# One of four heavy experts made light, with a new order of expert steps, the final norm ahead of the leftovers, and down-projections by column halves

## The chip, the cores and the metric

The kernel runs on one core of a Trainium2 chip. The metric is the device time of one execution in microseconds, the median of several runs. One more execution was taken with the hardware profiler; its trace gives the durations of single instructions, and its own time stands beside the runs below.

## The reference

Four residual blocks of a network on 256 tokens of width 1024 (float32): retention and a gated feed-forward layer, dilated attention and a second one, a mixed convolution and neighbourhood-attention layer with a third one, and a Fourier layer followed by a mixture of eight experts. A final norm ends it. The part that matters most here is the mixture:

```
logits = h @ w_router + b_router
top_val, top_idx = lax.top_k(logits, 2)            # 2 of 8 experts for each token
gate = softmax(top_val) at top_idx, 0 elsewhere
out = sum over e of gate[..., e] * ((silu(h @ w1[e]) * (h @ w3[e])) @ w2[e])
# w1[e], w3[e]: 1024 x 3584, w2[e]: 3584 x 1024
...
return x * rsqrt(mean(x * x) + 1e-6) * final_g     # after the residual
```

The weights of all eight experts, 352 MB, are read whichever tokens are routed to them.

## The kernel before

**Stages.** `core` runs the layers one after the other with `Net`'s helpers. Tokens are two blocks of 128 rows. Products that must be exact are made of three: a weight or activation is split into a high and a low part in a rounded format (`load` splits weights: ScalarE copies the high part, line 119, VectorE subtracts for the low part, line 120), and high x high, low x high and high x low are summed in PSUM. Every weight is loaded by `load` (line 110) on SyncE's DMA queue, in program order, into a ring of slots; a load waits until the slot's last reader is done.

**`down`** multiplies a hidden activation by the second matrix of a layer: two row blocks by two column halves, four PSUM tiles. The last `TB` = 5 blocks of 128 hidden columns are held back until the last weight is there, and then done row block by row block, with both column halves in turn for each weight. Seven layers' ends use it; four go on to a layer norm (`post_norm`), three to a gated residual with the statistics of the next norm (`gated_residual`).

**The experts.** After routing, tokens are gathered per expert by products with a selection matrix, and results are scattered back the same way. An expert has `FE` = 3584 hidden columns, cut into 7 steps of 512. A step is one `first` (products with w1 and w3, 2 MB each, in "wide" slots: `rawx` twice and `rawy` twice) and, one step later, one `back` (the product with w2, two loads of 1 MB, slots `raw` three times and `x` once). There are two kinds of step:

- *heavy*: a tile of 128 tokens; weights split in two; 48 products in `first` (line 1079), 24 in `back` (line 1119). Splits go into five buffers `w`.
- *light*: a tile of 64 tokens; weights unsplit, TensorE reads the loaded slots in float32: 32 products (line 1067) and 16 (line 1107).

`order_experts` ranks the experts by their number of tokens; expert 0 is always rank 0, since its weights must be asked for before the ranks are known. Ranks below `NH` = 4 are heavy, the others light. SyncE reads the ranks' expert numbers into registers (line 1255) and uses them for the addresses of all later loads. `plan` is the order of the 56 steps: the first two of expert 0, then light and heavy in turn, and light steps at the end. `rank` is called while step 1 is written.

A step with `u == 0` is a change of expert: the tokens of the next expert are gathered in `prepare`, and those of the expert before are scattered in `scatter`. If an expert has more tokens than its tile holds, the leftovers run after the plan: all eight experts again, behind one branch (`s.tc.If`, line 1380) that reads a count in each engine. The final norm and the stores come behind it.

Of the kernel before, what the change touches and what calls it, by code (L numbers as in the profile page):

```python
# [18 lines left out]
F32 = mybir.dt.float32  # L19
F32R = mybir.dt.float32r  # L20
I32 = mybir.dt.int32
AF = mybir.ActivationFunctionType
ALU = mybir.AluOpType
AX = mybir.AxisListType
PSUM = bass.MemoryType.PSUM
DRAM = bass.MemoryType.DRAM

D = 1024
T = 256
FF = 2816  # L30
NE = 8
NH = 4
FE = 3584
ALPHA = 4 ** 0.25
BIG = 1e30
TB = 5
# [16 lines left out]
class Net:  # L53
# [24 lines left out]
    def banks(s, mm, tp, aux):  # L78

        s.psx.close()  # L80
        s.ps, s.psn = s.pool("psum%d" % mm, 1, s.psx, space=PSUM), (mm, tp, aux)

    def mm_tile(s, shape, name="mm"):
        return s.ps.tile(shape, F32, name=name, tag="mm", bufs=s.psn[0])
# [95 lines left out]
    def down(s, x, name, base, nf):  # L180

        hh, hl = x
        po = [[s.mm_tile([128, 512]) for _ in range(2)] for _ in range(2)]
        w = []
        for f in range(nf):
            if f % 2 == 0:
                w += s.load(s.unit_r(name, base + f // 2))
            if f < nf - TB or f == nf - 1:  # L190
                fs = range(nf - TB, nf) if f == nf - 1 else [f]
                for t in range(2):
                    for g in fs:
                        wh, wl = w[g]
                        for i, (a, b) in enumerate(((hh, wh), (hl, wh), (hh, wl))):
                            for c in range(2):
                                s.nc.tensor.matmul(out=po[t][c], lhsT=a[:, g, t * 128:t * 128 + 128],
                                                   rhs=b[:, 0, c * 512:c * 512 + 512],
                                                   start=(g == 0 and i == 0), stop=(g == nf - 1 and i == 2))
        return po  # L200
# [814 lines left out]
    def experts(s, pc, m, plan, ss, rank=None):  # L1015
# [7 lines left out]
        nc = s.nc  # L1023
# [137 lines left out]
        for n, (r, light, _, u) in enumerate(plan):  # L1161
            P, x, po = ready[r]
            g = first(r, light, u, x)
            pms = next(g)
            hid = turn(last[1], last[3]) if last else None
            if pms is None:
                pms = next(g)
            if n == 1 and rank:
                rank()
                if order[True]:  # L1170
                    late = True
            if late is not None and order[late]:
                prepare(*order[late].pop(0))
            late = None
            if u == 6 and order[light]:
                if n + 1 < len(plan) and plan[n + 1][1] == light:
                    prepare(*order[light].pop(0))
                else:
                    late = light
            if last:  # L1180
                s.second(back, spread, scatter, last, hid, None)
            if u == 0:
                po.extend(s.mm_tile([128, 512]) for _ in range(1 if light else 2))
            rows = 64 if light else 128
            sg = s.np.tile([128, 512], F32, name="tm")
            nc.scalar.activation(out=sg[0:rows], in_=pms[0], func=AF.Silu)
            nc.vector.tensor_tensor(out=sg[0:rows], in0=sg[0:rows], in1=pms[1], op=ALU.mult)
            last = r, light, u, sg, po, P
# [34 lines left out]
    def order_experts(s, q, m, posm, gate, iota, tri8):  # L1223


        nc = s.nc
# [35 lines left out]
                nc.vector.tensor_copy(out[:, t, 1:NE], r[:, 1:NE])  # L1262
        cr = q.tile([128, NE], F32, name="cr")
        by_rank(cr, cn)
        nc.vector.tensor_scalar(out=cr[:, NH:NE], in0=cr[:, NH:NE], scalar1=64.0, scalar2=None, op0=ALU.add)
        cf = q.tile([128, 1], F32, name="cf")
        nc.vector.tensor_reduce(out=cf, in_=cr, axis=AX.X, op=ALU.max)
        nc.vector.tensor_copy(m.cnt, cf)
# [1 line left out]
    def moe(s, x):  # L1270
# [5 lines left out]
        with ExitStack() as ctx:  # L1276
# [15 lines left out]
            with ExitStack() as c2:  # L1292
# [63 lines left out]
                m.posm = pk.tile([128, 2, NE], F32, name="posr")  # L1356
                m.gate = pk.tile([128, 2, NE], F32, name="gater")
                m.cnt = pk.tile([128, 1], I32, name="cnt")
                m.idt = pk.tile([128, NE], I32, name="ids")
                m.counts = pk.tile([128, NE], F32, name="cn")  # L1360
                m.ids = [0]
# [5 lines left out]
            heavy = [(r, False, 0, u) for r in range(NH) for u in range(7)]  # L1367
            light = [(r, True, 0, u) for r in range(NH, NE) for u in range(7)]

            plan = heavy[:2]  # L1370
            for i in range(max(len(heavy) - 2, len(light))):
                plan += light[i:i + 1] + heavy[i + 2:i + 3]
            with ExitStack() as c2:
                pc = s.pool("moe_c", 1, c2)
                s.banks(5, 1, 2)
                s.experts(pc, m, plan, ss, lambda: s.order_experts(pc, m, posm, gate, iota, tri8))
            fg = pk.tile([128, D], F32, name="fg")
            nc.sync.dma_start(out=fg, in_=s.a["final_g"].to_broadcast([128, D]))
            n = nc.values_load(m.cnt[0:1, 0:1], min_val=0, max_val=256)
            with s.tc.If(n > 128):  # L1380

                with ExitStack() as c2:
                    s.experts(s.pool("moe_d", 1, c2), m, [(r, False, 128 if r < NH else 64, u) for r in range(NE)
                                                          for u in range(7)], ss)
            scales = [s.rms_scale(None, ss[:, t, :]) for t in range(2)]
            for t, rs in enumerate(scales):
                for c in range(2):
                    v = x[:, t, c * 512:c * 512 + 512]
                    f = fg[:, c * 512:c * 512 + 512]
                    if c == 0:  # L1390
                        nc.vector.scalar_tensor_tensor(out=v, in0=v, scalar=rs, in1=f, op0=ALU.mult, op1=ALU.mult)  # L1391
                    else:
                        nc.vector.tensor_tensor(out=v, in0=v, in1=f, op=ALU.mult)  # L1393
                        nc.scalar.activation(out=v, in_=v, func=AF.Copy, scale=rs)
            return x

    def store(s, x):
        for t in range(2):
# [9 lines left out]
def core(tc, a, out, stages=STAGES):  # L1408
    with ExitStack() as ctx:
# [20 lines left out]
        for k in stages:  # L1430
# [16 lines left out]
            if k == "ret":  # L1447
                x = s.retention(x, xt)
            elif k == "ffn0":
                x = s.ffn_first(x, xt, 0, filters="even" in stages)  # L1450
            elif k == "dil":
                x = s.dilated(x, xt)
            elif k == "ffn1":
                x = s.ffn_first(x, xt, 1, then, "even" in stages)
            elif k == "even":
                if not hasattr(s, "kc"):
                    with ExitStack() as c3:
                        for _ in s.context(c3):
                            pass
                if not hasattr(s, "spec"):  # L1460
                    with ExitStack() as c3:
                        for _ in s.hyena_filters(c3):
                            pass
                x = s.even_layer(x, xt, then)
                ckv.close()
            elif k == "ffn2":
                s.fourier_constants(s.pool("fou_c", 1, c2))
                x = s.ffn_second(x, xt, then)
            elif k == "fou":
                if "moe" in stages:  # L1470
                    s.moe_constants()
                if not hasattr(s, "cs"):
                    s.fourier_constants(s.pool("fou_c", 1, c2))
                x = s.fourier(x, xt, then)
            elif k == "moe":
                c2.close()
                if not s.wide:
                    s.moe_constants()
                x = s.moe(x)
        cln.close()  # L1480
        c2.close()
        s.store(x)

# [137 lines left out]
```

## Time and profile before

| what | us |
|---|---|
| median of 3 runs | 2315.69 |
| lowest and highest run | 2313.85, 2316.62 |
| the profiled execution | 2317.26 |
| its span in the trace | 2315.2 |
| TensorE busy in the span | 2236.4 (97%) |
| VectorE, ScalarE busy | 1486.4 (64%), 1072.7 (46%) |

The profiled execution is 0.07% above the median of the runs. The span is cut in 40 slices in the profile's page, 57.9 us each; the experts fill the slices from the 25th on. Times "from the span's start" count from the first instruction of the trace. The mean granted clock of TensorE in the span is 0.983 of full speed.

### The profile page before, as it was taken

How to read it: one execution, taken by the hardware profiler on the slowest of the kernel's cores; microseconds unless marked ns; L12 is line 12 of the kernel's file. 1: busy time of each engine (PE TensorE's matmuls, PEld its weight loads, DVE VectorE, ACT ScalarE, POOL GpSimd, SP SyncE). 2: the span in 40 equal slices, each digit the busy share in tenths (PEclk: the TensorE clock that was granted, in tenths of full speed). 3: DMA queues.
4: the chain of work that ended last, by engine and by line, in shares of the span. 5: the costliest groups of instructions: out<-in, count | busy, mean ns of one | idle time of the engine just before them, and what ended most of it. 6: DMA issues, size and time to landing. Idle time of an engine off the chain costs nothing. (4 is left out here: it accounts for less than half of the span.)

```text
span 2315.2 us, 34156 instructions
## 1 busy us (share of the span) xinstructions
PE 2236.4 (97%) x13729; PEld 1766.7 (76%) x13729; DVE 1486.4 (64%) x2024; ACT 1072.7 (46%) x1424; POOL 33.5 (1%) x39
## 2 busy tenths in 40 slices
PE   8999999999999999998899988999999999999997
PEld 8997998899997998986699877665566656656662
DVE  6987887867746655886655457555555655555553
ACT  4333444354445444645554345544444544444442
POOL 0000000000000000100000000000000000000000
PEclk9999999999999999999999997999999999999998
DMA  8666777777743555642355627899899989998994
GB/s 308 244 255 234 264 254 273 271 263 264 268 151 132 207 191 181 217 164 40 118 189 194 254 100 278 346 414 416 356 376 425 422 338 412 425 420 356 424 424 183
DMA packets 99712, 639.75 MB, mean 276 GB/s; under 512 B 22552, under 2 KB 33433, under 8 KB 39513
## 3 DMA queue, kind: packets, MB, share of 16 engines
q1 hardware_dynamic: 99128, 636.71, 71.6%
q8 instruction: 110, 1.80, 0.3%
q10 hardware_dynamic: 416, 0.78, 0.1%
q14 instruction: 58, 0.47, 0.1%
HBM read 634.17 MB, written 3.28 MB: 275 GB/s over the span
## 5 line engine op out<-in xcount | busy, mean ns | idle before, releaser
L119 ACT ACTIVATE wh<-raw 128x1024 fp32r<-128x1024 f32 x446 | 468.8, 1059 | 552.1 <-PE mm L160 256.8
L120 DVE TENSOR_TENSOR wl<-raw,wh 128x1024 fp32r<-128x1024 f32 x446 | 538.9, 1220 | 246.4 <-ACT wh L119 245.4
L160 PE MATMUL mm<-xTh,wh 128*128 128x256 f32 x1600 | 447.5, 280 | 0.7 <-ACT tm L825 0.7
L160 PE MATMUL mm<-xTh,wl 128*128 128x256 f32 x1600 | 446.5, 279 | 0.0
L160 PE MATMUL mm<-xTl,wh 128*128 128x256 f32 x1600 | 445.3, 278 | 0.0
L120 DVE TENSOR_TENSOR wl<-rawy,wh 128x1024 fp32r<-128x1024 f32 x216 | 255.6, 1222 | 87.1 <-ACT wh L119 86.5
L160 PEld LDWEIGHTS mm<-xTh,wh 128*128 128x128 f32 x1600 | 301.3, 188 | 7.7 <-issue 5.8
L160 PEld LDWEIGHTS mm<-xTh,wl 128*128 128x128 f32 x1600 | 300.8, 188 | 4.3 <-issue 4.3
L160 PEld LDWEIGHTS mm<-xTl,wh 128*128 128x128 f32 x1600 | 301.2, 188 | 3.3 <-issue 3.3
L119 ACT ACTIVATE wh<-rawy 128x1024 fp32r<-128x1024 f32 x216 | 224.1, 1057 | 52.3 <-PE mm L1079 27.9
L1067 PE MATMUL mm<-rawx,hx 128*64 128x512 f32 x864 | 202.7, 595 | 0.0
L1079 PE MATMUL mm<-wl,hgh 128*128 128x512 f32 x448 | 179.6, 402 | 4.1 <-DVE wl L120 4.1
L1079 PE MATMUL mm<-wh,hgh 128*128 128x512 f32 x448 | 181.1, 404 | 0.0
L1079 PE MATMUL mm<-wh,hgl 128*128 128x512 f32 x448 | 177.8, 397 | 0.0
L176 PE MATMUL mm<-wh,xTh 128*128 128x256 f32 x608 | 174.1, 288 | 2.8 <-ACT wh L119 2.4
L176 PE MATMUL mm<-wh,xTl 128*128 128x256 f32 x608 | 174.3, 287 | 1.5 <-DVE xTl L150 1.5
L176 PE MATMUL mm<-wl,xTh 128*128 128x256 f32 x608 | 173.9, 286 | 0.5 <-DVE wl L120 0.5
L1067 PEld LDWEIGHTS mm<-rawx,hx 128*64 128x64 f32 x864 | 62.3, 137 | 117.8 <-issue 117.3
L535 DVE CUSTOM_DVE_ANT_0 araw<-araw,cond 128x1024 f32<-128x1024 f32 x96 | 115.7, 1218 | 33.3 <-DMA araw<-in_w_ada_dram 33.2
L176 PEld LDWEIGHTS mm<-wh,xTh 128*128 128x128 f32 x608 | 118.3, 195 | 5.1 <-ACT wh L119 2.8
L176 PEld LDWEIGHTS mm<-wh,xTl 128*128 128x128 f32 x608 | 118.7, 195 | 2.8 <-DVE xTl L150 2.3
L176 PEld LDWEIGHTS mm<-wl,xTh 128*128 128x128 f32 x608 | 118.4, 195 | 1.5 <-DVE wl L120 1.0
(361 smaller groups left out, 3293.6 us busy)
## 6 DMA issues: line engine op xcount, KB each, us to landing
rawx<-in_moe_w_dram SPq DMA_DIRECT2D x56, 2048.0 KB, 11.3
rawy<-in_moe_w_dram SPq DMA_DIRECT2D x56, 2048.0 KB, 15.0
raw<-in_moe_w_dram SPq DMA_DIRECT2D x84, 1024.0 KB, 11.5
araw<-in_w_ada_dram SPq DMA_DIRECT2D x48, 1024.0 KB, 5.5
raw<-in_ffn_w_up_dram SPq DMA_DIRECT2D x44, 1024.0 KB, 4.8
raw<-in_attn_w_in_dram SPq DMA_DIRECT2D x36, 1024.0 KB, 5.0
raw<-in_ffn_w_dram SPq DMA_DIRECT2D x33, 1024.0 KB, 4.9
x<-in_moe_w_dram SPq DMA_DIRECT2D x28, 1024.0 KB, 8.2
```

Of the source, the lines that this page charges most:

```text
L119: nc.scalar.activation(out=h, in_=v, func=AF.Copy)
L120: nc.vector.tensor_tensor(out=l, in0=v, in1=h.bitcast(F32), op=ALU.subtract)
L160: s.nc.tensor.matmul(out=p[:, j, :], lhsT=a[:, kc, :], rhs=b[:, kc, :], start=n == 0, stop=n == 23)
L176: s.nc.tensor.matmul(out=p[:, tb if to is None else to, :], lhsT=a[:, kc, tb, :], rhs=b[:, kc % 4, :], start=n == 0, stop=n == 23)
L535: nc.vector.tensor_tensor_reduce(out=out, in0=r[:, j, :], in1=cond[src], scale=1.0, scalar=0.0, op0=ALU.mult, op1=ALU.add, accum_out=dst)
L1067: nc.tensor.matmul(out=ps[half], lhsT=x[:, kc, :], rhs=w[:, kc, :], start=kc == 0, stop=kc == 7)
L1079: nc.tensor.matmul(out=pm, lhsT=a[:, kc, :], rhs=b[:, kc % 2, :], start=n == 0, stop=n == 23)
```

## The change

Five edits. **(1)** `NH` goes from 4 to 3, so three experts are heavy and five light (21 and 35 steps). **(2)** `AHEAD` = 3: the first three steps of expert 0 stand at the head of the plan, `rank` is called one step later, and behind them the heavy steps are spread evenly among the light ones: three heavy, then light, light, heavy, and again (at two places light, heavy). **(3)** The final norm is a function `final` that writes a new tile `o` and stores it; it is called ahead of the branch. The branch's body now tests each expert for leftovers by itself (`m.over`, eight counts), and repeats the norm and the stores. The threshold allows 128 tokens in a heavy expert and 64 in a light one, as before. **(4)** In `down` the blocks that are held back are done column half by column half. **(5)** PSUM pools keep one name across stages and are reused with waits per tile.

```
-NH = 4
+NH = 3
+AHEAD = 3
...
-        s.ps, s.psn = s.pool("psum%d" % mm, 1, s.psx, space=PSUM), (mm, tp, aux)
+        s.ps, s.psn = s.pool("psum", 1, s.psx, space=PSUM, reuse_waits="tile"), (mm, tp, aux)
...
-                fs = range(nf - TB, nf) if f == nf - 1 else [f]
-                for t in range(2):
+                last = f == nf - 1
+                fs = range(nf - TB, nf) if last else [f]
+                for t, cs in ((t, cs) for t in range(2) for cs in (((0,), (1,)) if last else ((0, 1),))):
                     for g in fs:
                         wh, wl = w[g]
                         for i, (a, b) in enumerate(((hh, wh), (hl, wh), (hh, wl))):
-                            for c in range(2):
+                            for c in cs:
...
-            if n == 1 and rank:
+            if n == AHEAD - 1 and rank:
                 rank()
...
-        nc.vector.tensor_scalar(out=cr[:, NH:NE], in0=cr[:, NH:NE], scalar1=64.0, scalar2=None, op0=ALU.add)
+        nc.vector.tensor_scalar(out=cr[:, 0:NH], in0=cr[:, 0:NH], scalar1=128.0, scalar2=None, op0=ALU.add)
+        nc.vector.tensor_scalar(out=cr[:, NH:NE], in0=cr[:, NH:NE], scalar1=192.0, scalar2=None, op0=ALU.add)
+        nc.vector.tensor_copy(m.over, cr)
...
-            plan = heavy[:2]
-            for i in range(max(len(heavy) - 2, len(light))):
-                plan += light[i:i + 1] + heavy[i + 2:i + 3]
+            plan, rest, n = heavy[:AHEAD], heavy[AHEAD:], len(light)
+            for i in range(n):
+                plan += light[i:i + 1] + rest[i * len(rest) // n:(i + 1) * len(rest) // n]
...
-            n = nc.values_load(m.cnt[0:1, 0:1], min_val=0, max_val=256)
-            with s.tc.If(n > 128):
+            with ExitStack() as c2:
+                s.final(c2, x, [ss[:, t, :] for t in range(2)], fg)
+            n = nc.values_load(m.cnt[0:1, 0:1], min_val=0, max_val=512)
+            with s.tc.If(n > 256):
+                for r in range(NE):
+                    n = nc.values_load(m.over[0:1, r:r + 1], min_val=0, max_val=512)
+                    with s.tc.If(n > 256):
+                        with ExitStack() as c2:
+                            s.experts(s.pool("moe_d", 1, c2), m, [(r, False, 128 if r < NH else 64, u) for u in range(7)],
+                                      None)
                 with ExitStack() as c2:
-                    s.experts(...)
-            scales = [s.rms_scale(None, ss[:, t, :]) for t in range(2)]
...
+                    s.final(c2, x, [None, None], fg)
+
+    def final(s, ctx, x, ss, fg):
+        nc = s.nc
+        o = s.pool("fin", 1, ctx).tile([128, 2, D], F32, name="o")
+        scales = [s.rms_scale(x[:, t, :], ss[t]) for t in range(2)]
+        for t, rs in enumerate(scales):
+            for c in range(2):
+                cs = slice(c * 512, c * 512 + 512)
+                v, w, f = o[:, t, cs], x[:, t, cs], fg[:, cs]
+                if c == 0:
+                    nc.vector.scalar_tensor_tensor(out=v, in0=w, scalar=rs, in1=f, op0=ALU.mult, op1=ALU.mult)
+                else:
+                    nc.vector.tensor_tensor(out=v, in0=w, in1=f, op=ALU.mult)
+                    nc.scalar.activation(out=v, in_=v, func=AF.Copy, scale=rs)
+        s.store(o)
```

How VectorE's instructions stand in the middle of the expert stage, before. `wl` is the low part of a split weight from the slot named behind the arrow; `tm<-tm,mm` is the gated product of a step's two halves, 128 rows for a heavy step and 64 for a light one; `eTl` is the low part of a heavy step's turned activation.

```order
L1187 TENSOR_TENSOR tm<-tm,mm 64x512
L120 TENSOR_TENSOR wl<-rawy,wh 128x1024 x8
L1187 TENSOR_TENSOR tm<-tm,mm 128x512
L150 TENSOR_TENSOR eTl<-tp,eTh 128x512
L120 TENSOR_TENSOR wl<-raw,wh 128x1024 x2
L120 TENSOR_TENSOR wl<-x,wh 128x1024 x2
L1187 TENSOR_TENSOR tm<-tm,mm 64x512
L120 TENSOR_TENSOR wl<-rawy,wh 128x1024 x8
```

And in the change, at the same part of the stage:

```order
L1190 TENSOR_TENSOR tm<-tm,mm 64x512 x2
L121 TENSOR_TENSOR wl<-rawx,wh 128x1024 x8
L1190 TENSOR_TENSOR tm<-tm,mm 128x512
L151 TENSOR_TENSOR eTl<-tp,eTh 128x512
L121 TENSOR_TENSOR wl<-raw,wh 128x1024 x4
L1190 TENSOR_TENSOR tm<-tm,mm 64x512 x2
L121 TENSOR_TENSOR wl<-rawy,wh 128x1024 x8
```

Two light steps stand between two heavy ones, and the splits of a heavy step's weights take `rawx` and `rawy` in turn instead of `rawy` each time.

ScalarE's last instructions of the program's main path, before. `eTx` and `PT` belong to the last light step and its scatter, `ss` are the squares of the final norm.

```order
L1093 ACTIVATE eTx<-tp 128x256 x2
L1132 ACTIVATE PT<-tp 128x512
L149 ACTIVATE n<-tm 128x512
L567 ACTIVATE tp,ss<-x 128x512 x4
L1379 TENSOR_LOAD cnt
L1380 COMPARE_AND_BRANCH
```

In the change:

```order
L1135 ACTIVATE PT<-tp 128x2x128
L150 ACTIVATE n<-tm 128x512 x2
L570 ACTIVATE tp,ss<-x 128x512 x4
L1413 ACTIVATE o<-o,rs 128x512 x2
L1419 DMA out_dram<-o 128x512 x2
L1388 TENSOR_LOAD cnt
L1389 COMPARE_AND_BRANCH
```

The scaling of the output and its stores stand ahead of the count's load and the branch; before, they stood behind them. The last step is a heavy one.

TensorE in the `down` of the dilated attention, where the blocks that are held back begin, before. `mm_7433` and `mm_7434` are the two column halves of the first row block.

```order
L197 MATMUL mm_7433<-wh_7481,oTh_4293 128x512
L197 MATMUL mm_7434<-wh_7481,oTh_4293 128x512
L197 MATMUL mm_7433<-wh_7481,oTl_4294 128x512
L197 MATMUL mm_7434<-wh_7481,oTl_4294 128x512
L197 MATMUL mm_7433<-wl_7482,oTh_4293 128x512
L197 MATMUL mm_7434<-wl_7482,oTh_4293 128x512
```

In the change, around the place where the first column half ends:

```order
L200 MATMUL mm_7433<-wh_7517,oTh_4293 128x512
L200 MATMUL mm_7433<-wh_7517,oTl_4294 128x512
L200 MATMUL mm_7433<-wl_7518,oTh_4293 128x512
L200 MATMUL mm_7434<-wh_7481,oTh_4293 128x512
L200 MATMUL mm_7434<-wh_7481,oTl_4294 128x512
L200 MATMUL mm_7434<-wl_7482,oTh_4293 128x512
```

All 15 products of the first half stand ahead of the first product of the second.

## Rows read from the trace of the kernel before

**Rows 1.** The page: busy share of each engine; GB/s in 40 slices.

```profile
PE 2236.4 (97%) x13729; PEld 1766.7 (76%) x13729; DVE 1486.4 (64%) x2024; ACT 1072.7 (46%) x1424; POOL 33.5 (1%) x39
...
GB/s 308 244 255 234 264 254 273 271 263 264 268 151 132 207 191 181 217 164 40 118 189 194 254 100 278 346 414 416 356 376 425 422 338 412 425 420 356 424 424 183
```

**Rows 2.** Waits, 1400 to 2316 us: total us, times, longest us.

```profile
ACT wh L119 <- DMA raw<-in_moe_w_dram: 2.4, 1, 2.4
ACT wh L119 <- DMA x<-in_moe_w_dram: 0.5, 1, 0.5
...
SPq L110 <- DVE wl L120: 365.6, 64, 13.3
SPq L110 <- PE mm L1067: 203.6, 36, 10.6
SPq L1255 <- DVE ids L1254: 18.1, 1, 18.1
```

**Rows 3.** A stretch: length, busy PE, PEld, DVE, ACT, POOL; PE clock, DMA share, GB/s.

```profile
1735.28:1764.05 28.77, 28.77 (x129) 17.37 (x128) 16.14 (x15) 13.89 (x16) 0.00 (x0) 1.00 1.01 425
```

**Rows 4.** The stretch of rows 3, lines 1067, 1107, 1079, 1119 alone (PE, PEld).

```profile
1735.28:1764.05 28.77, 7.09 (x32) 2.21 (x32) 1.00 1.01 425
...
1735.28:1764.05 28.77, 3.65 (x16) 1.06 (x16) 1.00 1.01 425
...
1735.28:1764.05 28.77, 11.63 (x48) 8.94 (x48) 1.00 1.01 425
...
1735.28:1764.05 28.77, 5.87 (x24) 4.42 (x24) 1.00 1.01 425
```

**Rows 5.** Timeline of PE: first light step, its like 26 pairs later, end.

```profile
1451.54 7.09 PE L1067 MATMUL mm<-rawx,hx 128*64 128x512 f32 x32
...
2260.88 1.07 PE L1067 MATMUL mm<-rawx,hx 128*64 128x512 f32 x2
...
2295.37 1.89 PE L1107 MATMUL mm<-x,eTx 128*64 128x512 f32 x8
```

**Rows 6.** The page's DMA issues: KB each, median us from issue to landing.

```profile
rawx<-in_moe_w_dram SPq DMA_DIRECT2D x56, 2048.0 KB, 11.3
...
raw<-in_moe_w_dram SPq DMA_DIRECT2D x84, 1024.0 KB, 11.5
```

**Rows 7.** DMA, 1458.65 to 2280 us, and SyncE's timeline at its start.

```profile
DMA packets 30108, 328.20 MB, mean 400 GB/s; under 512 B 3337, under 2 KB 3337, under 8 KB 3436
...
1458.65 0.95 SPq L110 DMA_DIRECT2D rawx<-in_moe_w_dram  x2
```

**Rows 8.** Timeline of SyncE, and DMA issues at 1415.4 to 1415.8 us.

```profile
1742.39 0.92 SPq L110 DMA_DIRECT2D rawx<-in_moe_w_dram  x2
...
1415.53 0.36 SPq L110 DMA_DIRECT2D rawx<-in_moe_w_dram  x1
...
rawx<-in_moe_w_dram SPq DMA_DIRECT2D x1, 2048.0 KB, 7.7
```

**Rows 9.** A stretch as in rows 3, and PE's timeline in it.

```profile
1657.00:1671.00 14.00, 14.00 (x73) 9.35 (x72) 0.64 (x3) 1.85 (x4) 0.00 (x0) 0.88 0.98 400
...
1665.74 5.35 PE L1107 MATMUL mm<-raw,eTx 128*64 128x512 f32 x16
```

**Rows 10.** Timelines of DVE and PE behind two `down` calls.

```profile
1143.57 1.27 DVE L672 TENSOR_TENSOR x<-mm,grow 128x512 f32<-128x512 f32 x2
1144.77 1.27 DVE L673 TENSOR_TENSOR x<-x 128x512 f32<-128x512 f32 x2
...
1149.31 1.09 PE L596 MATMUL tp<-ident,n 128*128 128x128 f32 x4 [5.58 <-DVE n L593]
...
227.71 1.29 PE L213 MATMUL tp<-ident,x 128*128 128x128 f32 x8 [1.75 <-DVE x L247]
```

**Rows 11.** Timeline of the end: the last square and the first scale.

```profile
2304.27 0.19 ACT L567 ACTIVATION_READ_ACCUMULATOR tp<-x 128x1 f32 x1
...
2307.17 0.23 DVE L578 TENSOR_TENSOR rs<-ss 128x1 f32<-128x1 f32 x2 [3.53 <-ACTq L1380]
```

More of the change, by code (lines that the diff above doesn't have):

```diff
@@ L1358, in moe @@
                 m.cnt = pk.tile([128, 1], I32, name="cnt")
+                m.over = pk.tile([128, NE], I32, name="over")
                 m.idt = pk.tile([128, NE], I32, name="ids")
@@ L1378, in moe @@
             nc.sync.dma_start(out=fg, in_=s.a["final_g"].to_broadcast([128, D]))
-            n = nc.values_load(m.cnt[0:1, 0:1], min_val=0, max_val=256)
-            with s.tc.If(n > 128):
-                with ExitStack() as c2:
-                    s.experts(s.pool("moe_d", 1, c2), m, [(r, False, 128 if r < NH else 64, u) for r in range(NE)
-                                                          for u in range(7)], ss)
-            scales = [s.rms_scale(None, ss[:, t, :]) for t in range(2)]
@@ L1386, in moe @@
[L1386 to L1394, printed above, removed]
@@ L1395, in moe @@
-            return x
+            with ExitStack() as c2:
[8 more added lines that the diff above has]
+                                      None)
+                with ExitStack() as c2:
+                    s.final(c2, x, [None, None], fg)
@@ L1478, in core @@
                     s.moe_constants()
-                x = s.moe(x)
+                s.moe(x)
         cln.close()
         c2.close()
-        s.store(x)
 def _cols(w, c=256):
```

## The prediction

> **What bounds the kernel now.** I read four views, from coarse to fine. The page says that TensorE is busy in 97% of the span and that its last third, the experts, also moves the most bytes [rows 1]. So two resources are nearly full there, and the question is which one ends each step. The list of waits answers it [rows 2]: over the whole expert stage ScalarE, which splits heavy weights, waits for landings twice, 2.4 and 0.5 us, while SyncE, which issues the loads, waits 366 us for slots that VectorE's splits must free and 204 us for slots that light products must free. Loads wait for compute, not compute for loads: TensorE is the bound. A stretch [rows 3] shows how narrowly. One heavy and one light step take 28.77 us of unbroken TensorE work, and in the same stretch the DMA engines are at a share of 1.01 and 425 GB/s. A step loads 2 x 2.10 + 2 x 1.05 = 6.29 MB whether heavy or light [rows 6], so two steps need 12.58 MB / 425 GB/s = 29.6 us: 0.8 us more than the products. The kernel lives on loads made ahead and regains the lead at each change of expert, where TensorE loses time to gathers and scatters. DMA has very little left to give; that decides this forecast.
>
> **The change, part by part.** Sums are made against the profiled execution, 2317.26 us (span 2315.2); the median of the runs is 1.57 us lower, and results are stated on the median's scale at the end.
>
> *One expert from heavy to light.* A heavy step is 48 and 24 products, 11.63 + 5.87 us; a light one 32 and 16, 7.09 + 3.65 us [rows 4]. The difference is 6.76 us; with 28.77 us for both, heavy is 17.77 and light 11.00. Seven steps change kind: 47.3 us of TensorE work go. The expert's own gather and scatter stay as instructions of nearly the same number; I cost that difference at nothing. If TensorE stayed the bound, the last expert product (now ending at 2295.37 + 1.89 = 2297.3 [rows 5]) would end at 2250.
>
> *What DMA allows.* From 1458.65 us, when the fifth step's first load is issued, to 2280 us 328.2 MB were moved, a mean of 400 GB/s [rows 7]. At the 425 GB/s of a full stretch they take 772 us: the last load cannot land before about 2231, some 50 us earlier than now. That floor lies under 2250, but the two resources take turns. Three heavy in every nine steps: two light and one heavy step need 2 x 11.00 + 17.77 = 39.8 us of products and 3 x 14.80 = 44.4 us of loads. TensorE eats 4.6 us of its lead in three steps, 1.54 per step, and then waits. At a change of expert it gives lead back: from 1451.54 to 2260.88 us there are 26 pairs and six changes [rows 5], 809.3 - 26 x 28.77 = 61.3 us, so 10.2 us per change. The changes stay six; their cost is taken unchanged.
>
> How large can the lead be? A light step's two wide slots are given back when its products end: SyncE issues at 1742.39, the 7.09 us run that began at 1735.28 having just ended [rows 4, 8]. When such a step's second load lands, 8.39 MB of other loads have free slots and are queued, 19.7 us; the next needs those 7.1 us of products and then 7.7 us to landing on an idle queue, of which 4.9 is its own transfer [rows 8]. TensorE can be 19.7 - 7.1 - 2.8 = 9.8 us late before DMA idles. I take 9.8 as the full lead. Counting steps from 0, changes now come at steps 13, 17, 24, 34, 38 and 45 of 56, so stretches from step 3 on are 10, 4, 7, 10, 4, 7 and 10 steps, eating 15.4, 6.2, 10.8, 15.4, 6.2, 10.8 and 15.4 us. Starting each at a full lead, TensorE waits 5.6 us in each ten, 1.0 in each seven, nothing in the fours: 18.8 us. **The stage gains 47.3 - 18.8 = 28.5 us.** Bounds: 47 if the lead bridges everything, 9 if DMA idles as much as now (rivals).
>
> *Three first steps.* The third step becomes heavy; it is in the count of 21 and 35. Ranking gains three instructions on 128x8 tiles and stands one step later in the code, but VectorE's order has it as early as before. SyncE's 18.1 us wait for the ids [rows 2] now stands behind one more load; both are hidden by the first heavy products, whose splits free the next slot only at 1415.5 [rows 8]. Nothing, either way. The gain vector's 0.5 MB load moves from the end of the queue to its start, about 1.2 us of DMA at a time when it waits for slots. Waiting per PSUM tile instead of per pool: the first gather waits for its selection, not for a bank; nothing.
>
> *The end.* Today the squares end at 2304.46, and the next useful instruction, the scale, starts at 2307.17 after a wait of 3.53 us for the branch [rows 11]. Norm and stores now come ahead of the branch: 2304.46 to 2307.17 go, 2.7 us. The branch then runs under the stores' flight. If it doesn't fit under it, up to 2.7 come back; that end is zero. The last step is heavy now instead of light. From the last product to the last square it is 2304.46 - 2297.26 = 7.2 us today [rows 5, 11]; a heavy scatter works on two column halves, the first under the products of the second, a light one on two row blocks of one tile. I cost the difference at nothing; it cannot be more than a part of the 7.2, either way.
>
> *Column halves in `down`, seven calls.* The same products in another order: the first half of a row block is complete 15 products earlier. One eviction and one add or statistics pass, half of the 1.27 + 1.27 us pairs [rows 10], leave the path after the last product: 1.3 us, if someone waited. In the three calls that end in a gated residual TensorE does wait (5.58 us in one, [rows 10]); in the four that end in a layer norm next products cover most of it and 1.75 us or less are open. I take 3 x 1.3 + 4 x 0.3 = 5 us; the ends are 0 (VectorE busy with weight splits anyway) and 3 x 1.3 + 4 x 1.2 = 8.7.
>
> Sum: 28.5 + 2.7 + 5 = 36.2 us. 2317.26 - 36.2 = 2281.1; on the median's scale **2280 us**, 1.5% faster. With lead and halves at plausible ends (35 + 8 or 20 + 5 us), this case covers 2271 to 2289.
>
> **Rivals.** *The lead suffices.* If SyncE's order keeps more in flight than I count, TensorE never waits: 47.3 + 2.7 + 8 = 58 us, 2258. For it: hardly a landing is waited for now [rows 2]. Against: DMA is already at its full rate in undisturbed pairs [rows 3].
>
> *The clock falls at each wait.* Once in the present kernel the granted clock of a stretch is 0.88, after narrow gather products; the 16 light products behind them took 5.35 instead of 3.65 us [rows 9], part of them at 1.2 instead of 2.4 GHz: 1.7 us. If each of the 17 groups of three steps paid that once, TensorE would have 29 us more work: the product floor is 2250 + 29 = 2279, three steps need 41.5 us of the 44.4, ten steps eat only 9.8 us, and the waits vanish. The stage gains 18, the whole 26 us: 2290. For it: waits of about 5 us would be new. Against: a wait shorter than the loads' deficit costs nothing while loads bound. The Trainium skill, "TensorE: Matmul & The Clock Gate", section "HAM oscillation — how this bites in real kernels", speaks for this rival: a loop whose products per tile are shorter than the wait for the next weights pays the slow clock anew at every tile. The trace agrees that a disturbed stretch falls to half, but shows no wait for loads that does it.
>
> *DMA idles as now.* If slots come back as late at the changes as today, the 50 us of unused DMA stay, the last load lands at about 2280 again, and the last product ends some 8 us later (two splits, 12 products): 9 us gained in the stage, 2299. For it: the six changes remain. Against: TensorE reaches them with a smaller backlog.
>
> *Slower: the leftovers run.* A light expert holds 64 tokens, and the fourth rank is light now. Counting the reference's routing on the given inputs, expert 0 has 8 tokens and the others 118, 92, 64, 61, 58, 56, 55. The fourth is exactly 64; the test lets 64 pass. One token more and seven heavy steps follow after the first norm: 7 x 17.77 = 124 us, some 10 for loads not made ahead, 11 for the second norm and stores: 2425. It decides at 65. Against: the closest second and third logits of a token are 0.011 apart, far above rounding.
>
> On the rate itself: the undisturbed stretch moves 425 GB/s [rows 3]. The Trainium skill ("DMA: Bandwidth & Descriptors", section "Where 436 GB/s comes from") says that loads from HBM are held to about 358 GB/s. By that 328.2 MB would take an estimated 917 us, longer than now, and the change would gain nothing; the row decides.
>
> **How the numbers follow.** Forecast 0.60; lead suffices 0.12; clock 0.12; DMA idles 0.10; leftovers 0.03; something unforeseen without gain 0.03. The likeliest gives 2280. The range takes the forecast's whole width, the clock case and the case in which DMA idles as now; the lead that suffices and the last two cases, 0.18 together, stay outside: 2260 to 2300. Under about 0.2% a measurement of this kernel cannot be told from no change, 4.6 us. All cases but the last two are faster by more: 0.94; 0.02 same; 0.04 slower.
>
> **What would show it.** Right: 21 heavy and 35 light steps; weights' first readers (splits, light products) waiting for landings in steps before a change of expert and not behind one; the mean rate over the stage at 410 to 420 GB/s; the last expert load issued near 2235 to 2245; the scale following the squares at once; TensorE's 5.58 us gap down by about 1.3. Wrong: no wait for landings and the rate unchanged (slots bound), or a granted clock well under 0.97 in the stage.

## The result, and the profile after

The changed kernel takes **2288.83 us** (median of 4 runs, 2287.32 to 2295.14) where the kernel before took 2315.27 beside it; the ratio is 0.9889, interval [0.9872, 0.9907]. That is 26.4 us less; 36 were forecast, and the range (2260 to 2300) holds it. The profiled execution took 2287.32 us (span 2285.4, granted clock 0.984), the fastest of the four.

The page of the changed kernel, busy shares and GB/s, as in [rows 1]:

```profile
PE 2192.2 (96%) x13563; PEld 1698.5 (74%) x13563; DVE 1380.1 (60%) x1931; ACT 980.8 (43%) x1339; POOL 32.2 (1%) x39
...
GB/s 309 241 251 243 272 261 275 242 247 281 296 136 128 219 188 187 218 148 84 72 196 197 265 132 200 333 416 426 389 402 426 424 425 424 363 425 424 424 424 184
```

TensorE is busy 44 us less, and ten of the 13 slices before the last move 416 to 426 GB/s; the span is only 29.8 us shorter. Where each part went is read from the stretch between the first and the last expert product (columns as in [rows 3]), first of the kernel before:

```profile
1415.90:2297.30 881.40, 870.79 (x3889) 530.89 (x3889) 485.74 (x482) 406.56 (x477) 0.00 (x0) 0.99 0.94 388
```

and of the changed kernel:

```profile
1415.40:2268.90 853.50, 828.97 (x3723) 464.30 (x3723) 375.24 (x386) 316.63 (x392) 0.00 (x0) 0.99 0.95 398
```

| term | forecast, us | these two traces, us |
|---|---|---|
| TensorE's busy time in the stage | -47.3 | 870.79 to 828.97: -41.8 |
| TensorE's idle time in the stage | +18.8 | 10.61 to 24.53: +13.9 |
| the stage | -28.5 | 881.40 to 853.50: -27.9 |
| column halves: start of the stage | -5 | 1415.90 to 1415.40: -0.5 |
| last product to last square | 0 | 7.2 to 6.85: -0.3 |
| last square to end of the span | -2.7 | 10.74 to 9.65: -1.1 |

The stage came out within a microsecond of the forecast, in this execution. Both its terms are 5 us smaller than forecast, and that they cancel is luck, as the runs below show.

Who waits for a landing now (all engines, 1400 to 2286 us, and SyncE's queue), as in [rows 2]:

```profile
ACT wh L120 <- DMA raw<-in_moe_w_dram: 14.8, 7, 4.2
...
ACT wh L120 <- DMA rawy<-in_moe_w_dram: 12.2, 5, 6.3
...
ACT wh L120 <- DMA rawx<-in_moe_w_dram: 2.8, 2, 2.4
...
PE mm L1070 <- DMA rawx<-in_moe_w_dram: 1.3, 1, 1.3
...
PE mm L1070 <- DMA rawy<-in_moe_w_dram: 1.1, 1, 1.1
...
ACT wh L120 <- DMA x<-in_moe_w_dram: 1.0, 2, 0.5
...
SPq L111 <- PE mm L1070: 353.5, 51, 20.6
SPq L111 <- DVE wl L121: 175.2, 44, 9.5
```

Before, the splits waited 2.9 us for landings in all; now they wait 31 us, and TensorE itself 2.4 us. TensorE's two waits stand at 1907.23 and 2227.13 us. The first is at the end of the ten steps before the change at step 34, the second at the end of the last stretch: where the lead was to run out.

Landings are only a small part of what TensorE waits for. Its longest other waits between the first and the last expert product, of the kernel before:

```profile
PE mm L1079 <- DVE wl L120: 4.1, 3, 1.4
PE aux L1147 <- ACT n L149: 2.5, 4, 0.7
```

and of the changed kernel:

```profile
PE mm L1082 <- ACT wh L120: 4.7, 4, 1.5
PE aux L1150 <- ACT n L150: 4.1, 5, 1.5
PE mm L1082 <- DVE wl L121: 3.3, 7, 0.5
PE tp L1093 <- DVE tm L1190: 3.0, 2, 1.5
```

Of the 13.9 us more, 2.4 are waits for a landing, and 1.4 are waits for splits straight behind one (at 1889 to 1890 and at 2209.9 us). The other 10 are waits for work of ScalarE and VectorE: other splits, gated products, gathers and scatters.

### The profile page after: what moved, and what is told of

It is laid out like the page before. It is cut to its first block, busy times and chain, and to the rows that moved or that the text cites. A ratio compares the mean times of both kernels' runs of the same rounds, so it can differ in the third digit from the quotient of the medians.

```text
span 2285.4 us, 33482 instructions
## 1 busy us (share of the span) xinstructions
PE 2192.2 (96%) x13563; PEld 1698.5 (74%) x13563; DVE 1380.1 (60%) x1931; ACT 980.8 (43%) x1339; POOL 32.2 (1%) x39
## 4 chain that ended last, share of the span: by engine, by line
PE 83%; DVE 8%; DMA 5%; ACT 2%; issue 2%; POOL 0%; SPq 0%; ACTq 0%; DVEq 0%; POOLq 0%
PE mm L161 22%; PE mm L1070 12%; PE mm L200 11%; PE mm L1082 9%; PE mm L177 7%; PE mm L1122 5%; PE mm L1110 5%; DVE wl L121 3%; DMA araw<-in_w_ada_dram 2%; PE aux L1051 2%; PE tp L405 1%; PE mm L500 1%; DMA rawy<-in_moe_w_dram 1%; PE tp L1093 1%; DMA rawx<-in_moe_w_dram 1%
## 5 line engine op out<-in xcount | busy, mean ns | idle before, releaser
L1190 DVE TENSOR_TENSOR tm<-tm,mm 64x512 f32<-64x512 f32 (+1 forms) x56 | 38.1, 681 | 262.0 <-ACT tm L1189 205.1
L1070 PE MATMUL mm<-rawx,hx 128*64 128x512 f32 x576 | 140.9, 605 | 1.3 <-DMA rawx<-in_moe_w_dram 1.3
L1082 PE MATMUL mm<-wh,hgh 128*128 128x512 f32 x336 | 134.4, 400 | 4.8 <-ACT wh L120 4.7
L1082 PE MATMUL mm<-wl,hgh 128*128 128x512 f32 x336 | 132.9, 396 | 3.3 <-DVE wl L121 3.3
L538 DVE CUSTOM_DVE_ANT_0 araw<-araw,cond 128x1024 f32<-128x1024 f32 x96 | 115.9, 1220 | 29.8 <-DMA araw<-in_w_ada_dram 29.6
L1070 PE MATMUL mm<-rawy,hx 128*64 128x512 f32 x544 | 132.5, 602 | 1.1 <-DMA rawy<-in_moe_w_dram 1.1
L1082 PE MATMUL mm<-wh,hgl 128*128 128x512 f32 x336 | 132.4, 394 | 0.0
L121 DVE TENSOR_TENSOR wl<-rawy,wh 128x1024 fp32r<-128x1024 f32 x88 | 101.9, 1220 | 25.5 <-ACT wh L120 25.2
```

The costliest lines, as they stand in the source:

```text
L121: nc.vector.tensor_tensor(out=l, in0=v, in1=h.bitcast(F32), op=ALU.subtract)
L538: nc.vector.tensor_tensor_reduce(out=out, in0=r[:, j, :], in1=cond[src], scale=1.0, scalar=0.0, op0=ALU.mult, op1=ALU.add, accum_out=dst)
L1070: nc.tensor.matmul(out=ps[half], lhsT=x[:, kc, :], rhs=w[:, kc, :], start=kc == 0, stop=kc == 7)
L1082: nc.tensor.matmul(out=pm, lhsT=a[:, kc, :], rhs=b[:, kc % 2, :], start=n == 0, stop=n == 23)
```

## The experiments

**The edits one by one.** Each was made alone in the kernel before. The plan, edits (1) and (2) together:

```diff
-NH = 4
+NH = 3
+AHEAD = 3
...
+            plan, rest, n = heavy[:AHEAD], heavy[AHEAD:], len(light)
+            for i in range(n):
+                plan += light[i:i + 1] + rest[i * len(rest) // n:(i + 1) * len(rest) // n]
```

> The kernel before with three heavy experts and the new order of steps alone. The forecast on record: the stage gains 28.5 us, 2287 on the scale of 2315.3. Reading of the two traces: 881.4 - 853.5 = 27.9 us between first and last expert product, 2287. If instead the plan is worth its TensorE work (41.8 us less busy), 2273; if the other edits carry the gain, over 2300.

Measured: 2290.16 us (2288.84 to 2298.10), ratio 0.9889 [0.9874, 0.9905]. The plan alone gives as much as the whole change. Edit (5), the PSUM pools, was not run alone.

The column halves (the `for t, cs in ...` of `down`):

> The kernel before with only the column halves in the seven down-projections. The forecast on record: 5 us (0 to 8.7), 2310. Reading of the two traces: the first expert gather starts 0.5 us earlier, so 2315, not to be told from no change.

Measured: 2314.56, ratio 0.9997 [0.9988, 1.0006]: no change to be told, and not the 5 us (0.9978).

The end (`final` ahead of the branch, with the counts `m.over` and the tests by expert):

> The kernel before with only the final norm and the stores ahead of the branch. The forecast on record: 2.7 us, 2312.6. Reading of the two traces: from the last square to the end of the span 10.7 us became 9.65, so 1.1 us, 2314.2; the branch then stands behind the stores and is not covered by them.

Measured: 2305.34, ratio 0.9953 [0.9939, 0.9967]: 9 us less, which neither reading allows. The trace has the gain in the wrong place: the stage between first and last expert product, which this edit doesn't touch, went from 881.4 to 875.6 us. What the edit does touch there is an allocation: the counts take 32 bytes per partition, and the tiles allocated behind them, among them the gathered tokens (`hg`) and the turned activations (`eT`) of heavy steps, stand 32 bytes further on. So that alone was tried:

```diff
+                pk.tile([128, NE], I32, name="pad")
                 m.idt = pk.tile([128, NE], I32, name="ids")
```

> The kernel before with one unused tile of 32 bytes per partition where the changed kernel allocates its eight counts; nothing else. The run with the end alone gained 9.4 us, of which its own end explains 2: its heavy products follow each other every 229 to 231 ns instead of 231 to 237. If that comes from the operands of the heavy products standing 32 bytes further on in SBUF, this run gains about 7 us, 2308, with a pair of steps at 28.49 instead of 28.77 us. If it comes from anything else in that edit (what stands behind the branch, the order of the end), 2315.

Measured: 2305.28, beside 2312.85 of the kernel before, ratio 0.9964 [0.9952, 0.9976]: 7.6 us from an unused tile. A pair of steps in this run, and lines 1079 and 1119 alone in it, as in [rows 3, 4]:

```profile
1726.52:1755.01 28.49, 28.49 (x130) 17.38 (x129) 16.13 (x15) 13.86 (x16) 0.00 (x0) 1.00 1.01 424
...
1726.52:1755.01 28.49, 11.44 (x48) 8.94 (x48) 1.00 1.01 424
...
1726.52:1755.01 28.49, 5.78 (x24) 4.43 (x24) 1.00 1.01 424
```

The pair takes 28.49 instead of 28.77 us, all of it in the heavy products (11.44 + 5.78 instead of 11.63 + 5.87), at the same clock and with the same weight loads. This leaves the end itself about 2 us (ratio 0.9953 against 0.9964), which is not shown: the intervals overlap.

The other way round, the changed kernel without the shift (two small tiles, `mx` and `sm`, put into one):

> The changed kernel with two small tiles put into one, so that the operands of the heavy products stand where they stand in the kernel before. If the place matters: heavy products slower by some 5 ns, 21 x 72 x 5 = 7.6 us more TensorE work, of which the loads hide a part: 2290 to 2297. If it does not: 2289.

Measured: 2294.82 (2289.76 to 2296.94), ratio 0.9918 [0.9904, 0.9932], some 6 us slower than the change (0.9889), with intervals that only just touch. But the plan alone, which has no shift either, reached 0.9889. Executions of the changed kernel spread over 8 us, and their granted clock goes with it: 2287.32 us at 0.984, 2287.88 at 0.983, 2289.78 at 0.982, 2295.14 at 0.980. At the same four clocks the run without the shift took 2289.76, 2291.66, 2294.82 and 2295.80, 2296.94. That is 2 to 6 us for the 32 bytes in the changed kernel; nine executions suggest it and don't settle it.

**Does TensorE or do the loads decide now?** Two heavy experts instead of three:

```diff
-NH = 3
+NH = 2
...
-            with s.tc.If(n > 256):
+            with s.tc.If(n > 500):
```

> The changed kernel with two heavy experts and six light ones; the branch for leftovers is never taken, so 28 of the 92 tokens of the third rank are left out. If TensorE still bounds the stage, the seven steps give 7 x 5.63 = 39 us more: 2249. If DMA bounds it (the forecast), the last landing, now near 2251 in the trace, can come only as much earlier as DMA idles now, under 35 us, and each lead is eaten sooner: 2265 to 2282, with the rate over the stage at 415 to 425 GB/s and many more waits for landings on TensorE.

Measured: 2276.73, ratio 0.9837 [0.9822, 0.9852]: 12 us less than the change, not 39. TensorE's waits for landings in this run, and the stretch between its first and last expert product:

```profile
PE mm L1070 <- DMA rawx<-in_moe_w_dram: 15.5, 7, 3.5
...
PE mm L1070 <- DMA rawy<-in_moe_w_dram: 4.5, 5, 1.4
...
1407.17:2252.72 845.55, 797.82 (x3557) 403.70 (x3557) 271.68 (x291) 234.31 (x307) 0.00 (x0) 0.97 0.96 402
```

20 us instead of 2.4. TensorE is busy 31 us less than in the changed kernel and idle 23 us more, 18 of them for landings: with so little work on TensorE, the loads take over. The next run takes work from TensorE without touching the plan. In the changed kernel three steps (light, light, heavy) take 40.34 us; the stretch, and lines 1070, 1110, 1082 and 1122 alone:

```profile
1718.49:1758.83 40.34, 40.34 (x181) 21.40 (x181) 16.54 (x17) 14.64 (x19) 0.00 (x0) 1.00 1.01 424
...
1718.49:1758.83 40.34, 15.24 (x64) 4.60 (x64) 1.00 1.01 424
...
1718.49:1758.83 40.34, 8.10 (x33) 2.52 (x32) 1.00 1.01 424
...
1718.49:1758.83 40.34, 11.29 (x48) 8.94 (x48) 1.00 1.01 424
...
1718.49:1758.83 40.34, 5.79 (x24) 4.43 (x24) 1.00 1.01 424
```

64 products of line 1070 should take 2 x 7.09 = 14.18 us and 32 of line 1110 2 x 3.65 = 7.3 [rows 4]. The timeline shows the cut:

```profile
1746.99 1.07 PE L1070 MATMUL mm<-rawx,hx 128*64 128x512 f32 x2
1748.00 0.46 PE L1093 MATMUL tp<-ident,tm 64*128 64x64 f32 x4
1748.39 6.65 PE L1070 MATMUL mm<-rawx,hx 128*64 128x512 f32 x29
1754.45 0.64 PE L1110 MATMUL mm<-raw,eTx 128*64 128x512 f32 x1
```

Where a light step follows a light one, the transposes of the step before land behind the first pair of products. That pair takes 1.0 us instead of 0.44. They were put ahead of it:

```diff
+            early = last and light and last[1]
+            hid = turn(last[1], last[3]) if early else None
             g = first(r, light, u, x)
             pms = next(g)
-            hid = turn(last[1], last[3]) if last else None
+            if last and not early:
+                hid = turn(last[1], last[3])
```

> The changed kernel; where a light step follows a light step, the transposes of the step before stand ahead of its products instead of behind the first pair of them. Three steps took 40.34 us where the forecast had 39.8; the pair that is cut off took 1.0 us instead of 0.44. 17 light steps follow a light one: 17 x 0.57 = 9.7 us of TensorE work. If TensorE decides, 2279; if loads decide (the forecast), waits for landings grow by as much in the long stretches and the gain is 0 to 4, 2285 to 2289.

Measured: 2289.28, ratio 0.9898 [0.9883, 0.9913]: no gain. The three steps did become shorter, but not TensorE's busy time in the stage (second line):

```profile
1719.12:1758.44 39.32, 39.32 (x182) 21.05 (x180) 15.84 (x16) 14.04 (x19) 0.00 (x0) 1.00 1.01 426
...
1412.53:2270.56 858.03, 830.54 (x3723) 468.78 (x3723) 375.67 (x386) 316.98 (x392) 0.00 (x0) 0.98 0.95 396
```

The three steps take 39.32 us instead of 40.34, yet in the stage TensorE is busy 830.5 us where it was 829.0. Waits for landings took back 3 us: TensorE waits 5.6 us for them instead of 2.4, and its idle time is 27.5 us instead of 24.5. The larger part went to the granted clock, 0.980 in this trace and 0.984 in the changed kernel's: 0.004 x 2287 us is an estimated 9 us of full-speed time. Why it was lower stays open; all four executions have 0.980, and the clock is at 1.00 in the 8 us behind each of TensorE's six waits for a landing. So this run doesn't show which of TensorE and the loads decides. And from the other side, fewer bytes:

```diff
-                w1, w3 = [s.load(w, whole=True) for w in ws]
+                w1 = w3 = s.load(ws[0], whole=True)
```

> The changed kernel; light steps load w1 only and multiply with it twice, so w3 of the five light experts is left out: 73 of 352 MB less. Loads can't decide any more. What is left of the idle time is the price of the changes of expert. By the forecast the waits for loads are worth 18.8 us: 2270. By the trace (waits for landings on TensorE or on the splits in front of it, and the slow products behind them) 8 to 12: 2277 to 2281. If loads cost nothing: 2289.

Measured: 2268.45, ratio 0.9806 [0.9790, 0.9822], 19 us less than the change. In the two traces the stage is 15.6 us shorter:

```profile
1413.22:2251.16 837.94, 819.19 (x3723) 454.15 (x3723) 378.52 (x386) 323.14 (x392) 0.00 (x0) 0.99 0.79 318
```

Of these, 9.8 us are TensorE's busy time (819.2 instead of 829.0) and 5.8 its idle time. This run's order of TensorE's work is also free of the cut pairs, so the 19 us are not the price of the loads alone. Two heavy experts give a third of the 39 us and turn most of the rest into waits; fewer loads, in another order, give 19 us. **Both are nearly full in the changed kernel**: TensorE is busy in 97% of the stage, and the loads run at 411 GB/s up to the last one, where an undisturbed stretch moves 424 to 425. The loads take over when TensorE gets lighter still; that they alone decide in the changed kernel, as forecast, is not shown.

**Could the lead be used better?** Three tries, three misses. First, the order of the steps:

```diff
-AHEAD = 3
+AHEAD = 2
```

> The changed kernel with two first steps of expert 0 instead of three; the changes of expert then stand at steps 12, 19, 23, 34, 38, 45 instead of 13, 17, 24, 34, 38, 45. If loads decide between changes and DMA idles behind two changes that stand close together, the wider distance from the first to the second change makes DMA idle less: a step-by-step sum with the measured step times and a lead as in the forecast gives 7 to 11 us less, 2278 to 2282. If TensorE's work decides, the same work in another order, 2289.

Measured: 2290.01, ratio 0.9896 [0.9880, 0.9913]: no gain. Then a searched order, with the early transposes:

```diff
+            kinds = "HHHLLHLLHLHHLLLLLHLHHLHLHLLLHLLHLLLLLHHLHLHHHLLLLLLHLLLL"
+            plan = [heavy.pop(0) if k == "H" else light.pop(0) for k in kinds]
```

> The changed kernel with the transposes ahead of the products where a light step follows a light one, and with an order of the 56 steps searched with the same step-by-step sum: heavy steps are gathered ahead of the places where the lead is eaten, light ones stand behind a change, and four light steps at the end. If loads and the lead decide, 12 to 20 us less, 2269 to 2277. If the lead is not what decides, the same work as in the run with the early transposes, 2289.

Measured: 2293.46, ratio 0.9912 [0.9895, 0.9928]. The step-by-step sum, which had the stage's gain right, could not choose an order. The order did what it was made for: the splits wait 15 us for landings instead of 31, and none between 1704 us and the end. But where heavy steps stand next to each other, TensorE waits for the splits (8.7 us in this run, 4.7 in the changed kernel), which the sum undercounted. That is 4 us of the 16 to 24 that are missing. The granted clock is lower as well, 0.979 against 0.984 in the profiled executions, an estimated 11 us of full-speed time. Last, the same bytes in loads of half the size:

```diff
-                w1, w3 = [s.load(w, whole=True) for w in ws]
+                wq = [[s.load(w[:, i:i + 4, :], whole=True, wide=True) for w in ws] for i in (0, 4)]
...
-                w = s.load(src)
+                w = s.load(src[:, 0:4, :], wide=True) + s.load(src[:, 4:8, :], wide=True)
```

> The changed kernel with each 2 MB load of w1 and w3 made as two of 1 MB into two slots of half the size: the same bytes and the same room, but the first half of a slot comes free when half the products are done (3.5 us earlier in a light step), and products can start when the first half has landed (2.4 us earlier). If the lead of the loads is what the changed kernel lacks, the lead grows by 4 to 6 us, DMA idles less behind the changes of expert and the waits of the long stretches go: 2273 to 2282. If DMA already gives all it can, or the order of steps alone sets its idle time, 2289.

> The same halved loads in the kernel before. There TensorE hardly waits for a landing, so a longer lead is worth nothing: 2314, or a little more if twice the number of loads on SyncE costs anything. A gain of over 5 us here would say that the loads already bound the kernel before.

Measured: 2319.42, ratio 1.0019 [1.0009, 1.0030], and in the kernel before 2338.12, ratio 1.0091 [1.0076, 1.0106]: both some 24 to 30 us slower than without halving. The pair of steps in the second, and line 1119 alone in it:

```profile
1739.00:1768.83 29.83, 29.67 (x129) 17.23 (x128) 16.05 (x15) 13.54 (x16) 0.00 (x0) 1.00 1.01 419
...
1739.00:1768.83 29.83, 6.39 (x24) 4.28 (x24) 1.00 1.01 419
```

29.83 instead of 28.77 us, though TensorE waits for almost nothing: with other loads the scheduler also cut the transposes in pieces between products (6.39 instead of 5.87 us for the same 24), and the rate was 419 instead of 425 GB/s. 1.06 us in each of some 26 pairs would be 28 us; 24 were measured. So this run measured the cuts, not the lead. In the changed kernel with halved loads TensorE waits for no landing in the whole stage, but is busy 20 us more and waits 23 us for splits instead of 8. Whether a longer lead would help stays open; no version that does the whole work was found that beats the change.

## Why the prediction was right, point by point

*What bounds the kernel.* Right for the kernel before: a shift that shortens TensorE's products gave 7.6 us at once. Behind the change, "the two resources take turns" fits better than a bound by loads: TensorE's waits for landings are 2.4 us, and they reach 20 us only with one more expert made light.

*TensorE's work, 47.3 us.* Too large by 5.5 us. The step "heavy is 17.77 and light 11.00" held for a light step behind a heavy one. A light step behind a light one is new in this plan, and its first pair of products is cut. In the plan alone, where nothing is shifted, three such steps and the whole stage are

```profile
1726.02:1766.63 40.61, 40.61 (x182) 21.41 (x181) 16.55 (x17) 14.65 (x19) 0.00 (x0) 1.00 1.01 425
...
1416.46:2278.41 861.95, 838.47 (x3723) 466.79 (x3723) 375.21 (x386) 316.38 (x392) 0.00 (x0) 0.99 0.95 394
```

The three steps take 40.61 us instead of the 39.8 of the forecast. For all 17 such groups that is an estimated 14 us, and 47.3 - 14 = 33; the plan alone has 870.8 - 838.5 = 32.3 us less busy time in its stage. The shift, which the forecast didn't have, brings the changed kernel to 41.8: its trace has 829.0 us of busy time, that of the run without the shift 836.9. Part of these 8 us can be the clock (0.984 and 0.983). So the size was saved by a term that nobody had counted, which is luck.

*The waits, 18.8 us.* Right in place, wrong in size. They stand at the end of the second of the ten-step stretches and of the last one (1865 to 1912 and 2185 to 2242 us), and not behind a change; the first of the tens has none at its end, only two early on, at 1479 and 1501 us. (The last stretch has eleven steps, 45 to 55, where the forecast counted ten; by its own rule that is 1.5 us more.) The rate is as expected, and so is the last load:

```profile
DMA packets 29211, 318.84 MB, mean 411 GB/s; under 512 B 3239, under 2 KB 3239, under 8 KB 3239
...
2235.62 0.33 SPq L111 DMA_DIRECT2D x<-in_moe_w_dram  x1
```

(the first for 1458.65 to 2235 us). 411 GB/s instead of 400, where 410 to 420 stood; issued at 2235.6, where 2235 to 2245 stood. The size is mis-sized in two ways. "TensorE waits 5.6 us in each ten, 1.0 in each seven" came out at some 4 us in the whole stage, 2.4 for landings and 1.4 for splits behind them. Slower steps eat the lead more slowly, 44.4 - 40.34 = 4.1 us in three steps instead of 4.6; by the forecast's rule that still leaves an estimated 11, so the lead seems to be larger than the 9.8 us of the forecast. And 10 us more are waits for ScalarE and VectorE, which the forecast had at nothing when it took the changes' cost unchanged. That the idle time in all, 13.9 us more, is near 18.8 is luck.

*Column halves, 5 us.* Wrong: nothing that can be told. The step that failed is "1.3 us, if someone waited"; the end named for zero, "VectorE busy with weight splits anyway", is what happened. Behind the mixer's `down`, VectorE and then TensorE in the changed kernel:

```profile
1144.23 0.69 DVE L675 TENSOR_TENSOR x<-mm,grow 128x512 f32<-128x512 f32 x1
1144.84 0.40 DVE L610 TENSOR_SCALAR tm<-tp,mod 128x128 f32<-128x128 f32 x1
1145.15 0.68 DVE L676 TENSOR_TENSOR x<-x 128x512 f32<-128x512 f32 x1
1145.75 2.35 DVE L121 TENSOR_TENSOR wl<-raw,wh 128x1024 fp32r<-128x1024 f32 x2
1148.03 0.15 DVE L581 TENSOR_TENSOR rs<-ss 128x1 f32<-128x1 f32 x1
...
1149.92 1.09 PE L599 MATMUL tp<-ident,n 128*128 128x128 f32 x4 [5.56 <-DVE n L596]
```

The add ends 1145.83 - 1143.32 = 2.5 us behind the last product, where it took 1146.04 - 1142.68 = 3.4 before: 0.9 us earlier. Two weight splits (2.35 us) then stand ahead of the norm's statistics on the same engine, and TensorE waits 5.56 us where it waited 5.58 [rows 10].

*The end, 2.7 us.* The scale follows the squares at once:

```profile
2275.56 0.19 ACT L570 ACTIVATION_READ_ACCUMULATOR tp<-x 128x1 f32 x1
...
2276.08 0.15 DVE L581 TENSOR_TENSOR rs<-ss 128x1 f32<-128x1 f32 x1
...
2277.65 0.41 ACTq L1419 DMA_DIRECT2D out_dram<-o  x1
```

From the last square to the first store are now 1.9 us instead of 5.5, but from there to the end of the span 7.75 instead of 5.3: of the 3.6 us that go, 2.5 come back behind the stores, where the branch now stands. "That end is zero" was stated; the gain came out at 1.1 us in the trace; the runs leave about 2, which is not shown.

*The rivals.* The lead did not suffice, though it fell short by less than forecast. DMA does not idle as before (411 GB/s instead of 400). The leftovers did not run. The clock did not fall at TensorE's waits for loads in the changed kernel. The stretch of TensorE's second wait (1.28 us), and one of the gather at the change of step 34, as in [rows 9]:

```profile
2225.00:2234.20 9.20, 7.92 (x33) 2.26 (x31) 4.02 (x4) 4.49 (x5) 0.00 (x0) 1.00 1.01 425
...
1922.00:1930.00 8.00, 8.00 (x36) 6.82 (x38) 0.21 (x1) 0.95 (x3) 0.00 (x0) 0.55 1.03 432
```

The clock is at full speed through the wait, and near half in narrow gather products at the change of step 34, as before the change. But the waits here are short. In the run with two heavy experts, TensorE's four longest waits for landings and the 29 products behind each are

```profile
1554.76 8.35 PE L1070 MATMUL mm<-rawx,hx 128*64 128x512 f32 x29 [3.02 <-DMA rawx<-in_moe_w_dram]
...
2064.56 9.67 PE L1070 MATMUL mm<-rawx,hx 128*64 128x512 f32 x29 [3.46 <-DMA rawx<-in_moe_w_dram]
...
2153.21 8.02 PE L1070 MATMUL mm<-rawx,hx 128*64 128x512 f32 x29 [2.43 <-DMA rawx<-in_moe_w_dram]
...
2212.35 6.65 PE L1070 MATMUL mm<-rawx,hx 128*64 128x512 f32 x29 [3.44 <-DMA rawx<-in_moe_w_dram]
```

The granted clock in the 8 us from the first product on is 0.79, 0.62, 0.83 and 1.00; the same 29 products take 6.65 us in the changed kernel at full speed. So three of the four waits cost 1.4 to 3.0 us more than themselves. The rule cited for that rival (the Trainium skill, "TensorE: Matmul & The Clock Gate", section "HAM oscillation — how this bites in real kernels") was not at work in the changed kernel; with one more light expert the trace agrees with it at three waits of four. The clock still matters in the changed kernel, as its executions and the early transposes show, without a wait for a load behind it.

## What to carry to other kernels

Where two resources are nearly full, work taken from one is worth what the other has left, and the parts of a change don't add: alone, these were worth 25, 0 and 9 us, together 26. Before idle time is put down to one resource, sort it by what ended each wait; before a run without gain is, look at its busy time and its granted clock. A change of order brings neighbours that the old trace never shows (a light step behind a light one), so cost them from both sides. And an edit that gains in a stage that it doesn't touch deserves a run with nothing but its allocation.

## What the runs showed of the hardware

An unused tile of 32 bytes per partition made the kernel before 0.36% faster: 48 heavy products took 11.44 instead of 11.63 us with the tiles behind it 32 bytes further on. Which of the moved tiles it is, and why, was not tried. A pair of light products that is cut off by transposes takes 1.0 us instead of 0.44 at the same clock. With two heavy experts, TensorE's granted clock in the 8 us behind waits of 3.02, 3.46, 2.43 and 3.44 us for a landing was 0.79, 0.62, 0.83 and 1.00; behind the two waits of the changed kernel, 1.09 and 1.28 us, it was 1.00. Loads of 1 MB moved 419 GB/s in a stretch where loads of 2 MB and 1 MB mixed moved 424 to 425; but that stretch uses 12.58 MB in 29.83 us, 422 GB/s, so it doesn't show that smaller loads are slower.
